# A hybrid RWKV-7 and short-convolution layer on one core: transposes on VectorE and ScalarE, elementwise work on GpSimd, and the first masked product behind the last scan

## The chip, the cores and the metric

One Trainium2 chip, one of its cores. The metric is the time of one execution in microseconds, the median over several runs. A profiled execution gives the trace. TensorE is called PE (its weight loads PEld), VectorE DVE, ScalarE ACT, GpSimd POOL, and SyncE, which issues most DMAs, SP.

## The reference

One inference step of one layer. 128 context tokens and 256 latent tokens, 384 in all, go through a modulated RMSNorm and one wide projection. Branch A is RWKV-7 time mixing with 32 heads of 64 channels, once in each direction; branch B is a gated convolution of width 3. Both are gated, projected, merged and projected again, and added to the input.

```python
def step(S, inp):                      # branch A, per head and direction
    r_t, w_t, k_t, v_t, a_t, b_t = inp
    sa = jnp.einsum('dbhij,dbhj->dbhi', S, a_t)
    S = S * w_t[..., None, :] + sa[..., :, None] * b_t[..., None, :] + v_t[..., :, None] * k_t[..., None, :]
    y = jnp.einsum('dbhij,dbhj->dbhi', S, r_t)
    return S, y
...
y_a = (y.astype(h.dtype) * jax.nn.silu(g_a)) @ w_out_a
u = _conv3_rows(c_gate * x_b, conv_w, rows)
y_b = (b_gate * u * jax.nn.silu(g_b)) @ w_out_b
merged = jax.nn.sigmoid(m_a) * y_a + jax.nn.sigmoid(m_b) * y_b
return merged @ w_o, S_fin
```

The context scan starts from zero and its final states are outputs; the latent scan starts from given states.

## The kernel before, in words

**The dense products.** All of them are done in float32 as three matmuls (`mm3`, lines 81 to 83): high part of the weights by high and low part of the activations, low part of the weights by the high part. A `wload` brings a block of weights (8 x 128 rows by 256 columns) and `split` makes its parts in two quarters, q = 0 and 1: ACT copies the high part (line 88) and DVE subtracts for the low part (line 89), 128x1024 each. `whi` and `wlo` have three buffers, `raw` two. One quarter feeds eight units; a unit is one `mm3`, three matmuls. The object `ds_` is the stream of all these products, and `ds_.go(n)` puts n units into PE's order. PE's order is written out by hand; that of the other engines is set by the tile scheduler, with priorities (`high_priority`) and bounds (`issue_after`). What a generator `yield`s in the head loop is the number of units that `drive` puts behind it.

**The head loop.** It runs over 16 pairs of heads, b = 0 to 15, called heads here; 128 channels are on the partitions, and 160 units of the stream stand beside each head in the steady state. For each head:

- `prep_a(b)`: decay and rate by low-rank products, the squared norm of the keys (`pn`, `kn`). `prep_k(b)`: inverse norm (`kn`, reciprocals), running sums of the logarithmic decay (`L`, a scan instruction on DVE), their exponentials `ep` and `em`, the keys `kd` and `bn`. It is issued inside the scan of the head before, by `keys`, behind the corner copies `turn`.
- `prep_b(b)`: the products `pr` (receptance and key by decay) and `bk` (lines 675 and 676), 14 units, then the masked product: `pA = bk x pr` for 6 chunks of 64 tokens, 2 heads and 2 directions, multiplied by a mask on DVE into `A` (line 709). The diagonal 32x32 triangles of A go by DMA to DRAM (`ui`) and back as `U` with one triangle on each of 48 partitions, are inverted there by 30 steps of elimination on DVE (two operations each, lines 724 and 726), and go back the same way (`uo`) into A. `x11` holds turned 32x32 blocks of it (line 737). On GpSimd, `bk` is multiplied by the decay of its chunk (line 716).
- `prep_c(b)`: PE turns the values (`pv`, line 763, 3 transposes for each direction) and the decayed keys (`pb`, line 772, 10 in all), and ACT copies the results into `sav` (line 765) and `bt` (line 773). The given states are loaded and turned.
- `scan(b)`: the two corner products `pH` and `pX` that complete the inverse with x11 (lines 842 and following), then two chains of steps, the context in 2 and the latents in 4 chunks. A step is `po` (state by pr), a sum into sav on DVE, `pq` (A by sav), a copy on ACT, `pu` (bt by sav) and the new state `st` on DVE (line 831 for a first context state, 833 for the others). At the end `py2` gathers the outputs into `ytok`.
- `norm(b)` (group norm over ytok, on DVE with a square on ACT and a power on GpSimd) and `finish(b)` (three transposes `py` on PE, scale on ACT, bonus and gate on DVE, lines 939 and 940, a store).

`prep_a` of the next head stands behind `prep_c`; finish of the head before stands between pr, bk and the masked product.

Of the kernel before, what the change touches and what calls it, by code (L numbers as in the profile page):

```python
# [56 lines left out]
def hybrid_step(ctx, tc, cst, x_prompt, x_sample, state_f, state_b, c, c_ctx, ada_w, ada_b, norm_g,  # L57
# [27 lines left out]
    def split(src, shape, th, tl, pool, nm, rows=P):  # L85
        hi = pool.tile(shape, F32R, tag=th, name=f"{th}_{nm}")
        lo = pool.tile(shape, F32R, tag=tl, name=f"{tl}_{nm}")
        S.copy(hi[0:rows], src)  # L88
        V.tensor_tensor(lo[0:rows], src, hi[0:rows].bitcast(F32), ALU.subtract)  # L89
# [4 lines left out]
    PRO, WINDOW, FIRST, LAST = 32, 80, 24, 16  # L94

    def wload(view, k0, cols, nm):

        w = P * len(cols)
        raw = wp.tile([P, 8, w], F32, tag="raw", name=f"raw_{nm}", bufs=2)
        if cols[-1] == cols[0] + P:  # L100
            nc.sync.dma_start(raw[:], view[:, k0:k0 + 8, cols[0]:cols[0] + 256])
        else:
            for i, c0 in enumerate(cols):
                nc.sync.dma_start(raw[:, :, i * P:(i + 1) * P], view[:, k0:k0 + 8, c0:c0 + P])
        res = [split(raw[:, 4 * q:4 * q + 4, :], [P, 4, w], "whi", "wlo", wp, f"{nm}_{q}") for q in range(2)]
        return res
# [501 lines left out]
    def prep_a(b, o):  # L608
# [58 lines left out]
    def prep_b(b, o):  # L667

        r, kk = r_[b], o["kk"]
        o["pr"], o["bk"] = [], []  # L670
        for d in range(2):
            ep, em, kd, bn = o["ep"][d], o["em"][d], o["kd"][d], o["bn"][d]
            pr = sp.tile([P, NCH, P], F32, tag=f"pr{d}", name=f"pr_{b}_{d}")
            bk = sp.tile([P, NCH, P], F32, tag=f"bk{d}", name=f"bk_{b}_{d}")
            V.tensor_tensor(bk[:, :, 0:C], c3(bn[:]), c3(em[:]), ALU.mult)
            V.tensor_tensor(bk[:, :, C:P], c3(kd[:]), c3(em[:]), ALU.mult)
# [20 lines left out]
        for d in range(2):  # L697
# [7 lines left out]
            for n0, w in ((0, 4), (4, 2)):  # L705
                mk = cs[:, m0:m0 + P].rearrange("p (w t) -> p w t", t=C).unsqueeze(1).broadcast_to([P, w, 2, C])
                for h in range(2):
                    f0 = NCH * d + n0
                    V.tensor_tensor(A[:, :, f0:f0 + w, hss[h]].rearrange("p w n t -> p n w t"),
                                    pas[h, n0][:, 0:w, :].rearrange("p n (w t) -> p n w t", t=C), mk, ALU.mult)  # L710
# [4 lines left out]
        for d in range(2):  # L715
            G.tensor_tensor(o["bk"][d][:], o["bk"][d][:], o["ep"][d][:, :, C:C + 1].broadcast_to([P, NCH, P]), ALU.mult)
# [19 lines left out]
        for d in range(2):  # L736
            box["turned"] = V.transpose(x11[0:32, 12 * d:12 * d + 12, :], blocks(A, d, 0)).ins

    def prep_c(b, o):

        r, v, A = r_[b], v_[b], o["A"]
# [9 lines left out]

        sav = sp.tile([P, 2 * NCH, P], F32, tag="sav", name=f"sav_{b}")
        bt = sp.tile([P, 2 * NCH, P], F32, tag="bt", name=f"bt_{b}")
        o["sav"], o["bkt"] = sav, bt
        for d in range(2):
            if d == 0:
                src = v
            else:
                src = tmp(f"vr_{b}")
                S.copy(src[:], v[:, ::-1])  # L760
            pv = bank(f"pv_{b}_{d}")
            for q in range(3):
                TE.transpose(pv[:, q, :], src[:, q * P:(q + 1) * P], ident)
            for e in range(2):
                S.copy(sav[C:P, NCH * d + e:NCH * d + NCH:2, :], pv[C * e:C * e + C, 0:3, :])
            yield 1
        for d in range(2):

            for n0, n1 in (((0, 4), (4, 5)), ((0, 3), (4, 6)))[d]:
                pb = bank(f"pb_{b}_{d}_{n0}")  # L770
                for n in range(n0, n1):
                    TE.transpose(pb[:, n - n0, :], o["bk"][d][:, n, :], ident)
                S.copy(bt[:, NCH * d + n0:NCH * d + n1, :], pb[:, 0:n1 - n0, :])
                yield 1
# [9 lines left out]
    def scan(b, o):  # L784
# [7 lines left out]
        def chain(ch):  # L792
            ls = None
            for i in range((2, 4)[ch]):
# [30 lines left out]
                if need_state:  # L825
# [3 lines left out]
                    for hs in hss:  # L829
                        if zero:  # L830
                            V.tensor_copy(st[ch][hs, :, hs], pu[hs, 0:2, hs])
                        else:
                            V.tensor_tensor(st[ch][hs, :, hs], pu[hs, 0:2, hs], ls[hs, :, hs], ALU.add)
# [125 lines left out]
    prep_k(0, cur)  # L959
    prev = None  # L960
    for b in range(NB):
# [210 lines left out]
```

## Time and profile before

| | us |
|---|---|
| median of 3 runs | 2238.54 |
| lowest and highest run | 2236.75, 2238.73 |
| the profiled execution, its own time | 2234.36 |
| its span in the trace | 2232.6 |
| PE busy in the span | 2173.1 |
| DVE busy | 1553.3 |
| ACT busy | 1013.5 |
| POOL busy | 115.7 |

The mean granted clock of PE was 0.998. Busy times of different engines overlap, so they don't add up to the span; matmul records overlap one another too, so a matmul's cost to PE is the distance from its start to the next one's. A row of the timeline gives the start and the duration in us, the engine, the line, the operation, what it writes and reads, and its shape; several instructions of one kind that follow one another are one row (x2, x3), and what is in brackets is the engine's idle time before it and what ended it. A row of the groups gives the count, the busy time in all and the mean of one in ns, and the engine's idle time before them.

### The profile page before, as it was taken

The numbers are of one execution on the slowest core, as the hardware profiler recorded it, in microseconds if no ns is written. First come the engines' busy times: TensorE is split into PE (matmuls) and PEld (weight loads), VectorE is DVE, ScalarE is ACT, GpSimd is POOL, SyncE is SP. The second block draws the span as 40 slices with busy tenths as digits, with TensorE's granted clock in tenths as the row PEclk, the third lists the DMA queues.
The fourth block names the chain that finished last, engine by engine and source line by source line (L and its number), as shares of the span: only waits on it lengthen the run. The fifth ranks groups of instructions, "written<-read, shape, count | busy, mean of one in ns | idle before, by whom it ended". The sixth has DMA issues, their size and how long they took to land.

```text
span 2232.6 us, 40518 instructions
## 1 busy us (share of the span) xinstructions
PE 2173.1 (97%) x16020; PEld 2062.7 (92%) x16020; DVE 1553.3 (70%) x3240; ACT 1013.5 (45%) x1784; POOL 115.7 (5%) x113
## 2 busy tenths in 40 slices
PE   5999999999999999999999999999999999999998
PEld 3589999999999999999999999999999999998988
DVE  3259567787878878777878787887777785444354
ACT  4245435454545454444445454546454633333333
POOL 2000000000000000000000000000000000000000
PEclk9999999999999999999999999999999999999999
DMA  9974454444343435343444434344445464886633
GB/s 338 346 211 128 131 141 116 116 117 118 108 132 107 130 100 131 106 130 100 121 108 127 112 107 133 107 122 126 124 118 139 144 196 143 294 281 233 220 132 113
DMA packets 426574, 335.25 MB, mean 150 GB/s; under 512 B 82496, under 2 KB 408720, under 8 KB 425488
## 3 DMA queue, kind: packets, MB, share of 16 engines
q1 hardware_dynamic: 424896, 330.91, 50.2%
q8 instruction: 126, 2.06, 0.4%
q10 hardware_dynamic: 432, 1.57, 0.2%
q14 instruction: 64, 0.52, 0.1%
q0 software_dynamic: 1056, 0.19, 0.1%
HBM read 305.80 MB, written 26.21 MB: 149 GB/s over the span
## 4 chain that ended last, share of the span: by engine, by line
PE 74%; DVE 12%; DMA 6%; ACT 4%; issue 2%; SPq 1%; POOL 0%; POOLq 0%; DVEq 0%; ACTq 0%
DMA raw_adah<-in_ada_w_dram 4%; PE d_rk L81 3%; PE d_rk L82 3%; PE d_rk L83 3%; PE d_gv L81 3%; PE d_gv L82 3%; PE d_gv L83 3%; PE d_oa L81 2%; PE pA L703 2%; PE d_oa L83 2%; PE d_oa L82 2%; PE d_mb L81 2%; PE d_mb L83 2%; PE d_mb L82 2%; PE d_bc L81 2%
## 5 line engine op out<-in xcount | busy, mean ns | idle before, releaser
L724 DVE TENSOR_TENSOR ut<-U 48x30 f32<-48x30 f32 (+14 forms) x480 | 154.8, 323 | 18.3 <-DMA U<-ui 5.5
L81 PE MATMUL d_rk<-h_hi,whi_rk 128*128 128x384 f32 x480 | 161.7, 337 | 0.6 <-ACT lst L554 0.6
L726 DVE TENSOR_TENSOR U<-U,ut 48x30 f32<-48x30 f32 (+14 forms) x480 | 154.5, 322 | 11.1
L81 PE MATMUL d_gv<-h_hi,whi_gv 128*128 128x384 f32 x480 | 160.6, 335 | 0.0
L82 PE MATMUL d_rk<-h_lo,whi_rk 128*128 128x384 f32 x480 | 160.5, 334 | 0.0
L83 PE MATMUL d_rk<-h_hi,wlo_rk 128*128 128x384 f32 x480 | 160.4, 334 | 0.0
L83 PE MATMUL d_gv<-h_hi,wlo_gv 128*128 128x384 f32 x480 | 160.4, 334 | 0.0
L82 PE MATMUL d_gv<-h_lo,whi_gv 128*128 128x384 f32 x480 | 160.4, 334 | 0.0
L88 ACT CAST whi_gv<-raw_gv 128x1024 fp32r<-128x1024 f32 (+1 forms) x64 | 64.0, 999 | 139.6 <-PE d_rk L82 100.0
L88 ACT CAST whi_rk<-raw_rk 128x1024 fp32r<-128x1024 f32 x60 | 63.0, 1054 | 110.8 <-PE d_rk L82 34.7
L89 DVE TENSOR_TENSOR wlo_rk<-raw_rk,whi_rk 128x1024 fp32r<-128x1024 f32 x60 | 72.9, 1218 | 45.3 <-ACT whi_rk L88 35.6
L81 PE MATMUL d_bc<-h_hi,whi_bc 128*128 128x384 f32 x256 | 92.2, 360 | 0.0
L81 PE MATMUL d_gb<-h_hi,whi_gb 128*128 128x384 f32 x256 | 92.2, 360 | 0.0
L81 PE MATMUL d_bg<-h_hi,whi_bg 128*128 128x384 f32 x256 | 92.2, 360 | 0.0
L81 PE MATMUL d_bx<-h_hi,whi_bx 128*128 128x384 f32 x256 | 92.1, 360 | 0.0
L81 PE MATMUL d_ma<-h_hi,whi_ma 128*128 128x384 f32 x256 | 91.6, 358 | 0.0
L81 PEld LDWEIGHTS d_rk<-h_hi,whi_rk 128*128 128x128 f32 x480 | 90.1, 188 | 0.9 <-ACT lst L554 0.9
L81 PE MATMUL d_mb<-h_hi,whi_mb 128*128 128x384 f32 x256 | 90.4, 353 | 0.0
L81 PEld LDWEIGHTS d_gv<-h_hi,whi_gv 128*128 128x128 f32 x480 | 90.1, 188 | 0.2
L81 PE MATMUL d_ob<-ybh,whi_ob 128*128 128x384 f32 x256 | 88.4, 345 | 2.0 <-DVE smb L521 1.0
L82 PEld LDWEIGHTS d_rk<-h_lo,whi_rk 128*128 128x128 f32 x480 | 90.2, 188 | 0.0
L82 PEld LDWEIGHTS d_gv<-h_lo,whi_gv 128*128 128x128 f32 x480 | 90.1, 188 | 0.0
(315 smaller groups left out, 6548.4 us busy)
## 6 DMA issues: line engine op xcount, KB each, us to landing
raw_adah<-in_ada_w_dram SPq DMA_DIRECT2D x64, 512.0 KB, 8.7
raw_rk<-in_w_in_dram SPq DMA_DIRECT2D x60, 512.0 KB, 5.3
raw_gv<-in_w_in_dram SPq DMA_DIRECT2D x60, 512.0 KB, 4.9
raw_ma<-in_w_in_dram SPq DMA_DIRECT2D x16, 1024.0 KB, 5.6
raw_mb<-in_w_in_dram SPq DMA_DIRECT2D x16, 1024.0 KB, 5.6
raw_bc<-in_w_in_dram SPq DMA_DIRECT2D x16, 1024.0 KB, 5.5
raw_bx<-in_w_in_dram SPq DMA_DIRECT2D x16, 1024.0 KB, 5.4
raw_bg<-in_w_in_dram SPq DMA_DIRECT2D x16, 1024.0 KB, 5.5
```

The source lines that it names most:

```text
L81: TE.matmul(out, wh, xh, start=start, stop=False)
L82: TE.matmul(out, wh, xl, start=False, stop=False)
L83: TE.matmul(out, wl, xh, start=False, stop=stop)
L88: S.copy(hi[0:rows], src)
L89: V.tensor_tensor(lo[0:rows], src, hi[0:rows].bitcast(F32), ALU.subtract)
L703: TE.matmul(pas[h, n // 4 * 4][:, n % 4, :], bk[hss[h], n, :], pr[hss[h], n, :], start=True, stop=True)
L724: V.tensor_tensor(tv, U[:, 0:s, s:s + 1].broadcast_to([48, s, w]), U[:, s:s + 1, s + 1:].broadcast_to([48, s, w]), ALU.mult)
L726: V.tensor_tensor(U[:, 0:s, s + 1:], U[:, 0:s, s + 1:], tv, ALU.add)
```

## The change

1. **Values.** `prep_v` turns v on DVE in 32x32 blocks (two instructions, 128x384), and 16 ACT copies of 32x192 put the blocks where they belong in sav. The transposes `pv` on PE, their copies and the copy of the reversed v are gone.
2. **Keys.** After GpSimd's decay, DVE turns bk in place in 32x32 blocks (two of 128x768), and 32 ACT copies of 32x192 place the blocks in bt. The transposes `pb` are gone.
3. **Low parts.** The second quarter (q = 1) of each wload has its low part made by GpSimd.
4. **Keys' decay.** `prep_p` makes the two halves of bk (by em) on GpSimd, for all heads but the first, issued behind the keys in the scan of the head before.
5. **pr** has two buffers; `prep_r` and `prep_v` of the next head are issued in the scan, behind the context chain's last state (`st0`).
6. **Joined.** The 14 units between pr and the masked product, and the one behind py2, are gone from the loop, so the next head's first masked product follows py2 directly. The norm of the head before is issued behind the masks, and 10 units and its finish follow the masked products.
7. **x11** shares one tile with U, and its turning is issued in the next head's prep_a.

```diff
+    def split(src, shape, th, tl, pool, nm, rows=P, eng=V):
...
-        V.tensor_tensor(lo[0:rows], src, hi[0:rows].bitcast(F32), ALU.subtract)
+        eng.tensor_tensor(lo[0:rows], src, hi[0:rows].bitcast(F32), ALU.subtract)
...
-    PRO, WINDOW, FIRST, LAST = 32, 80, 24, 16
+    PRO, WINDOW, FIRST, LAST, NRM = 32, 80, 24, 30, 10
...
-        res = [split(..., f"{nm}_{q}") for q in range(2)]
+        res = [split(..., f"{nm}_{q}", eng=(V, G)[q]) for q in range(2)]
...
+    def prep_v(b, o):
+        o["vt"] = []
+        for d in range(2):
+            x = sp.tile([P, T], F32, tag=f"vt{d}", name=f"vt_{b}_{d}")
+            V.transpose(x[:], v_[b][:, ::-1] if d else v_[b][:])
+            o["vt"].append(x)
+    def prep_p(b, o):
+        eng = G if b else V
...
+            eng.tensor_tensor(bk[:, :, 0:C], c3(o["bn"][d][:]), c3(o["em"][d][:]), ALU.mult)
+            eng.tensor_tensor(bk[:, :, C:P], c3(o["kd"][d][:]), c3(o["em"][d][:]), ALU.mult)
...
-        yield PB0
...
+        with tc.issue_after(last):
+            for d in range(2):
+                V.transpose(flat(o["bk"][d][:]), flat(o["bk"][d][:]))
...
+        ux = sp.tile([112, 1024], F32, tag="ux", name=f"ux_{b}")
+        U = ux[64:112].rearrange("p (a b) -> p a b", b=32)
...
+        for d in range(2):
+            for p in range(4):
+                for q in range(4):
+                    S.copy(bt[32 * p:32 * p + 32, NCH * d:NCH * d + NCH, 32 * q:32 * q + 32],
+                           o["bk"][d][32 * q:32 * q + 32, :, 32 * p:32 * p + 32])
+                yield 6
+        for d in range(2):
+            x = o["vt"][d][:].rearrange("p (n e t) -> p n e t", e=2, t=32)
+            for e in range(2):
+                for q in range(4):
+                    S.copy(sav[C + 32 * e:C + 32 * e + 32, NCH * d:NCH * d + NCH, 32 * q:32 * q + 32],
+                           x[32 * q:32 * q + 32, :, e, :])
+                yield 6
...
-        yield 1
+        yield 0
         V.tensor_tensor(ytok[:], ytok[:], py[:, 0:3, :], ALU.add)
...
         pb_gen = prep_b(b, cur)
-        ds_.go(next(pb_gen))
+        for d in range(2):
+            ds_.go(next(pb_gen))
         if prev is not None:
+            norm(b - 1, prev, cur["masked"])
+        drive(pb_gen)
+        n = 0
+        if prev is not None:
+            ds_.go(NRM)
+            n = NRM
             finish(b - 1, prev)
-        drive(pb_gen)
-        n = drive(prep_c(b, cur))
+        n += drive(prep_c(b, cur))
...
+        def values():
+            with tc.issue_after(cur["st0"]):
+                prep_r(b + 1, nxt)
+                prep_v(b + 1, nxt)
+        late = ((lambda: all(cur.get("turn", (None,))), keys), (lambda: "st0" in cur, values))
```

What stands in a row on the engines, by the order in which they get their instructions (a number behind a name is that of its buffer or its use):

On DVE, in a scan of the steady state, from the reciprocals of the next head's keys on. Before:

```order
L646 RECIPROCAL kn_7955<-kn_7955 128x128 x3
L654 SCALAR_TENSOR_TENSOR L_0_8105<-cs,sig_0_7896 128x384
L89 TENSOR_TENSOR wlo_bc_0_1_8046<-raw_bc_0_8039,whi_bc_0_1_8045 128x1024
L831 COPY st_1144<-pu_0_0_8143 64x2x64 x2
L647 SCALAR_TENSOR_TENSOR kn_7955<-kk_7860,kn_7955 128x384
L659 TENSOR_SCALAR kd_0_8109<-sig_2_7932,par,omka 128x384
L833 TENSOR_TENSOR st_1146<-pu_1_0_8159,ls_1_0_8031 64x2x64 x2
```

And now:

```order
L653 RECIPROCAL kn_8079<-kn_8079 128x128 x3
L661 SCALAR_TENSOR_TENSOR L_0_8231<-cs,sig_0_8020 128x384
L654 SCALAR_TENSOR_TENSOR kn_8079<-kk_7984,kn_8079 128x384
L666 TENSOR_SCALAR kd_0_8235<-sig_2_8056,par,omka 128x384
L661 SCALAR_TENSOR_TENSOR L_1_8239<-cs,sig_1_8032 128x384
L859 COPY st_1144<-pu_0_0_8275 64x2x64 x2
L667 TENSOR_TENSOR kd_0_8235<-k_7822,kd_0_8235 128x384
L668 TENSOR_TENSOR sig_2_8056<-kn_8079,sig_2_8056 128x384
L861 TENSOR_TENSOR st_1146<-pu_1_0_8291,ls_1_0_8157 64x2x64 x2
```

The low part of bc has left DVE, and the product of kn, kd and the second scan of the decay have moved ahead of the copies of the first context state.

On PE, at the end of that scan, where py2 (here py_5) gathers the outputs. Before:

```order
L82 MATMUL d_bc_1_8200<-h_lo_83,whi_bc_1_1_8207 128x384
L83 MATMUL d_bc_1_8200<-h_hi_79,wlo_bc_1_1_8208 128x384
L898 MATMUL py_5_8371<-sav_7533,A_7358 64x64 x24
L81 MATMUL d_bx_0_8396<-h_hi_76,whi_bx_0_0_8295 128x384
L82 MATMUL d_bx_0_8396<-h_lo_80,whi_bx_0_0_8295 128x384
```

And now:

```order
L82 MATMUL d_bc_1_8332<-h_lo_83,whi_bc_1_1_8339 128x384
L83 MATMUL d_bc_1_8332<-h_hi_79,wlo_bc_1_1_8340 128x384
L927 MATMUL py_5_8513<-sav_7499,A_7389 64x64 x24
L726 MATMUL pA_0_0_0_8555<-pr_0_8382,bk_0_8247 128x128
L726 MATMUL pA_0_1_0_8556<-pr_0_8382,bk_0_8247 128x128
```

The masked product of the next head has moved up to py2; it stood 15 units further on, behind the finish of the head before.

On GpSimd, from the decay of one head's bk to the clearing of A in its scan. Before:

```order
L716 TENSOR_TENSOR bk_1_7300<-bk_1_7300,ep_1154 128x768
L863 MEMSET A_7358 64x1536
L929 TENSOR_TENSOR rs_8434<-var_8431,nhalf 128x6
L716 TENSOR_TENSOR bk_0_8438<-bk_0_8438,ep_1148 128x768
L716 TENSOR_TENSOR bk_1_8444<-bk_1_8444,ep_1150 128x768
L863 MEMSET A_8502 64x1536
```

And now:

```order
L741 TENSOR_TENSOR bk_0_8247<-bk_0_8247,ep_1148 128x768
L741 TENSOR_TENSOR bk_1_8250<-bk_1_8250,ep_1150 128x768
L89 TENSOR_TENSOR wlo_bx_1_1_8584<-raw_bx_1_8577,whi_bx_1_1_8583 128x1024
L959 TENSOR_TENSOR rs_8654<-var_8651,nhalf 128x6
L89 TENSOR_TENSOR wlo_rk_0_1_8754<-raw_rk_0_8746,whi_rk_0_1_8753 128x1024
L89 TENSOR_TENSOR wlo_rk_1_1_8861<-raw_rk_1_8853,whi_rk_1_1_8860 128x1024
L89 TENSOR_TENSOR wlo_gv_0_1_8932<-raw_gv_0_8924,whi_gv_0_1_8931 128x1024
L89 TENSOR_TENSOR wlo_gv_1_1_9017<-raw_gv_1_9009,whi_gv_1_1_9016 128x1024
L89 TENSOR_TENSOR wlo_bg_0_1_9087<-raw_bg_0_9080,whi_bg_0_1_9086 128x1024
L89 TENSOR_TENSOR wlo_bg_1_1_9184<-raw_bg_1_9177,whi_bg_1_1_9183 128x1024
L892 MEMSET A_8554 64x1536
```

Seven low parts now stand on GpSimd between the decay and the clearing of A, around the power of the norm.

More of the change, by code (lines that the diff above doesn't have):

```diff
@@ L104, in wload @@
                 nc.sync.dma_start(raw[:, :, i * P:(i + 1) * P], view[:, k0:k0 + 8, c0:c0 + P])
-        res = [split(raw[:, 4 * q:4 * q + 4, :], [P, 4, w], "whi", "wlo", wp, f"{nm}_{q}") for q in range(2)]
+        res = [split(raw[:, 4 * q:4 * q + 4, :], [P, 4, w], "whi", "wlo", wp, f"{nm}_{q}", eng=(V, G)[q])
+               for q in range(2)]
         return res
@@ L636, in prep_a @@
         kn = sp.tile([P, T], F32, tag="kn", name=f"kn_{b}")
-        with tc.issue_after(box["turned"]) if "turned" in box else ExitStack():
+        if p is not None:
+            with tc.issue_after(lws):
+                p["turn_x"]()
+        with tc.issue_after(box["turned"]) if p is not None else ExitStack():
             box["kn"] = V.tensor_scalar(kn[:], pn, 1e-24, None, ALU.max).ins
@@ L734, in prep_b, with turn @@
                 nc.sync.dma_start(blocks(A, d, e), uo[d, e].rearrange("i s t -> s i t"))
-        for d in range(2):
-            box["turned"] = V.transpose(x11[0:32, 12 * d:12 * d + 12, :], blocks(A, d, 0)).ins
+        def turn():
+            for d in range(2):
+                box["turned"] = V.transpose(x11[0:32, 12 * d:12 * d + 12, :], blocks(A, d, 0)).ins
+        o["turn_x"] = turn
     def prep_c(b, o):
-        r, v, A = r_[b], v_[b], o["A"]
+        r = r_[b]
         s_in = sp.tile([P, 2, C], F32, tag="s_in", name=f"s_in_{b}")
@@ L750, in prep_c @@
                                       [:, :, 32 * jb:32 * jb + 32])
[L752 to L765, printed above, removed]
-            yield 1
[L767 to L774, printed above, removed]
         ks = o["kd"]
@@ L779, in prep_c @@
         yield 1
+        sav, bt = o["sav"], o["bkt"]
+        for d in range(2):
[4 more added lines that the diff above has]
+                yield 6
+        for d in range(2):
+            x = o["vt"][d][:].rearrange("p (n e t) -> p n e t", e=2, t=32)
[4 more added lines that the diff above has]
+                yield 6
         for h in range(2):
@@ L913, in scan, with norm @@
                                       nst[p0:p0 + 32, d, :].rearrange("i (b j) -> i b j", j=32))
-    def norm(b, o):
+    def norm(b, o, masked=None):
         ytok = o["ytok"]
@@ L919, in norm @@
         mu = sp.tile([P, 6], F32, tag="mu", name=f"mu_{b}")
-        V.tensor_reduce(mu[:], y6, AX.X, ALU.add)
+        with tc.issue_after(masked) if masked is not None else ExitStack():
+            V.tensor_reduce(mu[:], y6, AX.X, ALU.add)
         V.tensor_scalar(mu[:], mu[:], 1.0 / C, None, ALU.mult)
@@ L941, in finish, with drive @@
         nc.sync.dma_start(ya_d[b], ya[:])
-    def drive(gen, prio=0, at=None, fn=None):
-        n = i = 0
+    def drive(gen, prio=0, late=()):
+        n = 0
+        late = list(late)
         while True:
-            if i == at:
-                fn()
-            i += 1
+            for x in [x for x in late if x[0]()]:
+                x[1]()
+                late.remove(x)
             with tc.high_priority(offset=prio):
@@ L951, in drive @@
             if u is None:
+                assert not late
                 return n
@@ L967, in hybrid_step @@
         pb_gen = prep_b(b, cur)
-        ds_.go(next(pb_gen))
+        for d in range(2):
+            ds_.go(next(pb_gen))
         if prev is not None:
+            norm(b - 1, prev, cur["masked"])
+        drive(pb_gen)
+        n = 0
+        if prev is not None:
+            ds_.go(NRM)
+            n = NRM
             finish(b - 1, prev)
-        drive(pb_gen)
-        n = drive(prep_c(b, cur))
+        n += drive(prep_c(b, cur))
         nxt = {}
+        w = WINDOW + (FIRST if b == 0 else LAST if b == NB - 1 else 0)
         if b < NB - 1:
@@ L986, in keys @@
                 prep_k(b + 1, nxt)
-        drive(scan(b, cur), 300, 3 if b < NB - 1 else None, keys)
-        norm(b, cur)
+                prep_p(b + 1, nxt)
+        def values():
[3 more added lines that the diff above has]
+        late = ((lambda: all(cur.get("turn", (None,))), keys), (lambda: "st0" in cur, values))
+        drive(scan(b, cur), 300, late if b < NB - 1 else ())
         prev, cur = cur, nxt
+    norm(NB - 1, prev)
     ds_.go(12)
```

56 lines of the change are left out of this document (34 added, 22 removed).

## Prediction

> **What bounds the kernel now.** I read the page's busy shares and chain first, then stretches of the window view, then PE's waits inside the recurrence, and last the timelines of the stages that the change touches.
>
> ```profile
> span 2232.6 us, 40518 instructions
> PE 2173.1 (97%) x16020; PEld 2062.7 (92%) x16020; DVE 1553.3 (70%) x3240; ACT 1013.5 (45%) x1784; POOL 115.7 (5%) x113
> PE 74%; DVE 12%; DMA 6%; ACT 4%; issue 2%; SPq 1%; POOL 0%; POOLq 0%; DVEq 0%; ACTq 0%
> 600.00:800.00 200.00, 198.41 (x1574) 193.75 (x1573) 158.41 (x349) 92.69 (x166) 11.41 (x8) 1.00 0.43 116
> 746.08:775.33 29.25, 29.25 (x170) 29.25 (x170) 27.73 (x76) 11.27 (x14) 0.00 (x0) 1.00 0.39 112
> PE po L804 <- DVE st L833: 6.0, 8, 0.8
> PE pu L828 <- ACT sav L823: 1.2, 5, 0.3
> PE pq L821 <- DVE sav L805: 0.8, 2, 0.4
> ```
>
> PE is the bound: busy 97% of the span at a granted clock of 1.00, and 74% of the chain. In the middle of the head loop (the 200 us window; columns are length, then PE, PEld, DVE, ACT, POOL busy) it idles 1.6 us in 200. So an instruction taken from PE is time saved, and a wait put on PE is time lost. The last three rows are PE's waits in the scans between 300 and 1700 us, some thirteen heads: 8.0 us, 0.6 a head. DVE is no bound on average (79% of that window), but in the 29.25 us in which one head's triangular elimination runs it is busy 27.73 us, 95%: there is little room there for a DVE that is held up. POOL does nothing in that stretch.
>
> **Term 1: 16 transposes a head leave PE.**
>
> ```profile
> 737.18 0.33 PE L81 MATMUL d_bg<-h_hi,whi_bg 128*128 128x384 f32 x1
> 739.26 0.49 PE L763 MATMUL pv<-cs,v 128*128 128x128 f32 x3
> 743.81 0.34 PE L82 MATMUL d_rk<-h_lo,whi_rk 128*128 128x384 f32 x1
> ```
>
> Starts are pipelined, so a matmul costs its pitch and not its duration. From 737.18 to the first transpose at 739.26 stand 12 main matmuls: 2.08/12 = 0.1733 us each. From there to 743.81 stand all 16 transposes and 16 main matmuls: 4.55 - 16 x 0.1733 = 1.78 us. Sixteen heads make 28.4 us. PE's other work stays. Certain, if nothing else waits: **-28.4**.
>
> **What comes in its place on DVE, ACT and GpSimd.** The rows by line (count, busy us, mean ns):
>
> ```profile
> L716 POOL TENSOR_TENSOR bk<-bk,ep 128x768 f32<-128x768 f32 x32 | 49.3, 1541 | 155.6 <-PE pA L703 140.9 <-DMA ui<-A 10.1 <-issue 4.6
> L89 DVE TENSOR_TENSOR wlo_rk<-raw_rk,whi_rk 128x1024 fp32r<-128x1024 f32 x60 | 72.9, 1218 | 45.3 <-ACT whi_rk L88 35.6 <-DMA ma_d<-ma 4.5 <-DMA mb_d<-mb 4.5
> L676 DVE TENSOR_TENSOR bk<-kd,sig 128x384 f32<-128x384 f32 x32 | 17.5, 548 | 0.1
> L675 DVE TENSOR_TENSOR bk<-sig,sig 128x384 f32<-128x384 f32 x32 | 17.5, 548 | 0.0
> L737 DVE STREAM_TRANSPOSE x<-A 32x384 f32<-32x384 f32 x32 | 17.4, 558 | 25.3 <-DMA A<-uo 25.1
> L855 ACT COPY x<-pH 32x192 f32<-32x192 f32 x32 | 9.9, 311 | 46.6 <-PE pH L842 39.9 <-DVE x L855 6.7
> L765 ACT COPY sav<-pv 64x384 f32<-64x384 f32 x64 | 30.3, 474 | 15.0 <-PE pv L763 14.1
> L760 ACT COPY vr<-v 128x384 f32<-128x384 f32 x16 | 8.0, 502 | 0.0
> ```
>
> DVE turns: a turn of 384 columns took 0.558; taken by columns, two of 768 and two of 384 make 2 x 1.12 + 2 x 0.56 = 3.3 us a head. DVE gives up ten low parts (12.2 us) and four products (2.2 us), so it is 11 us lighter a head of 105. ACT: 48 copies of 32x192 at 0.311 = 14.9 us, less the sav copies (4 x 0.474) and vr (0.502), the old bt copies not counted: at most +12.5 us a head, from 46% of the window to 58%. The copies come in groups of four (1.2 us) with 6 units (3.1 us of PE) behind each, and at least 16 units of the next head's first preparation follow the last, so 8.3 us cover it. Cost taken: 0; with that cover gone, 1.2 us a head, 19 in all.
>
> GpSimd: no row shows its low part. Its 768-column product took 1.48 us at best (row below), 1.97 for 1024 columns; below it stands 1.22, DVE's own. I take 1.97. Ten low parts, four products and the two decays come to 10 x 1.97 + 4 x 0.74 + 2 x 1.54 = 26 us a head: far from a bound by itself.
>
> [...]
>
> **Who shuts out whom.** What the pages of groups don't show is that the two engines exclude one another:
>
> ```profile
> 185.25 1.48 POOL L716 TENSOR_TENSOR bk<-bk,ep 128x768 f32<-128x768 f32 x1 [36.71 <-PE pA L703]
> 185.66 3.28 DVE L89 TENSOR_TENSOR wlo_ma<-raw_ma,whi_ma 128x1024 fp32r<-128x1024 f32 x2
> 304.59 1.49 POOL L716 TENSOR_TENSOR bk<-bk,ep 128x768 f32<-128x768 f32 x1 [5.21 <-PE pA L703]
> 304.62 0.68 DVE L709 TENSOR_TENSOR A<-pA,cs 128x512 f32<-128x512 f32 x1
> 305.22 1.27 DVE L940 TENSOR_TENSOR ya<-ya,ga 128x384 f32<-128x384 f32 x1
> 191.37 2.38 POOL L716 TENSOR_TENSOR bk<-bk,ep 128x768 f32<-128x768 f32 x1 [4.65 <-issue]
> ```
>
> Two low parts took 3.28 instead of 2 x 1.22 where POOL was running; the ya product 1.27, where such a product takes 0.55, so it began at about 305.94, 0.14 before POOL's recorded end. The masked product, which reads PSUM, took 0.68 beside POOL and wasn't held. And a POOL product that came second took 2.38 instead of 1.48. So a DVE operation with two operands in SBUF and a POOL operation wait for one another, whole instructions long.
>
> [...]
>
> Per low part moved DVE gains 1.22 and may lose 1.97 - 0.14 = 1.83. Where DVE has slack that is nothing. Two places have none.
>
> **Term 2: the scan.** The first scan steps of head 5, with the next head's keys already on DVE:
>
> ```profile
> 794.76 2.55 DVE L646 RECIPROCAL kn<-kn 128x128 f32<-128x128 f32 x3
> 796.32 1.05 ACT L88 CAST whi_bc<-raw_bc 128x1024 fp32r<-128x1024 f32 x1 [0.27 <-PE d_gb L82]
> 797.25 0.88 DVE L654 TENSOR_TENSOR_SCAN L<-cs,sig 128x384 f32<-128x384 f32 x1
> 798.06 1.19 DVE L89 TENSOR_TENSOR wlo_bc<-raw_bc,whi_bc 128x1024 fp32r<-128x1024 f32 x1
> 799.27 0.59 DVE L831 COPY st<-pu 64x128 f32<-64x128 f32 x2
> 799.90 0.56 DVE L647 SCALAR_TENSOR_TENSOR kn<-kk,kn 128x384 f32<-128x384 f32 x1
> 800.37 0.48 DVE L659 TENSOR_SCALAR kd<-sig,par,omka 128x384 f32<-128x384 f32 x1
> 800.78 0.60 PE L804 MATMUL po<-st,pr 128*128 128x128 f32 x4
> ```
>
> This low part is one of those moved. Its cast ends at 797.37; GpSimd starts when the L scan lets go, at about 798.0, and holds till 798.0 + 1.97 - 0.14 = 799.8. In the new order of DVE the kn product, kd and the second L scan stand ahead of the state copies. kn has two SBUF operands, so it starts at 799.8; then by pitches 0.47 + 0.51 + 0.81 + 0.62 to the end of the copies: 802.2. po, for which PE wants the states, stands at 800.78: 1.4 us of PE waiting. What is behind po on PE is the feed, so it all waits. Fourteen heads have this order (the first has another feed, the last no next head): **+19.6**. Bounds: 0, if GpSimd got in earlier or kn isn't held, to 2 us x 15 = 30, had it to run after the kn product too. The rows above speak for holding.
>
> The second place is the r products and v turns behind the context's last state: 4 x 0.55 + 2 x 0.56 = 3.3 us of DVE, which the next sav add may find in its way by up to 0.5 us. Before's own waits there (0.6 us a head) came from the kd and bn products that now run elsewhere. **0**, bounds -8 and +8.
>
> **Term 3: the elimination.** From the mask to the corner product pH, head 5 and then head 4:
>
> ```profile
> 735.68 1.95 DVE L709 TENSOR_TENSOR A<-pA,cs 128x512 f32<-128x512 f32 x4 [0.65 <-PE pA L703]
> 746.08 0.18 DVE L724 TENSOR_TENSOR ut<-U 48x30 f32<-48x30 f32 x1 [0.30 <-DMA U<-ui]
> 775.12 0.20 DVE L726 TENSOR_TENSOR U<-U,ut 48x30 f32<-48x30 f32 x1
> 782.78 1.14 DVE L737 STREAM_TRANSPOSE x<-A 32x384 f32<-32x384 f32 x2 [1.40 <-DMA A<-uo]
> 787.37 0.62 PE L842 MATMUL pH<-x,A 32*32 32x32 f32 x48
> 681.65 1.02 DVE L737 STREAM_TRANSPOSE x<-A 32x384 f32<-32x384 f32 x2 [2.15 <-DMA A<-uo]
> 682.37 0.76 PE L842 MATMUL pH<-x,A 32*32 32x32 f32 x48
> ```
>
> Masked at 737.63, U ready to use at 746.08 (8.45 later), eliminated at 775.32, back and turned at 783.92; pH at 787.37, a slack of 3.4 us. Head 4 has none: pH begins as the second turn ends. In the new order the mask comes 15 units earlier before the scan (14 of the feed, one of the last scan): +7.8, less the 1.78 of transposes, plus 0.3 for finish's transposes, now inside: +6.3 us of time. Against it: the norm and the ya products now stand ahead of U, by which I let it start 1.9 us later (bounds 0 and 4); the bk turns, 2.2; four low parts leave DVE, -4.9; four or five GpSimd low parts block it, 4.4 x 1.83 less the DVE idle of 1.5 already there: +6.6. Together 5.8 against 6.3: the slacks stay about what they are. The three heads with none (4, 8 and 15 by the same two rows) take 1 us each: **+3**, bounds 0 and +15.
>
> The norm now runs behind the mask, and finish's transposes 10 units behind; the norm's eight steps, at 0.55 as the products above, take some 5 us, and 16 units from the first masked product (8.3 us) are there. 0, and 0.5 us a head if they are late.
>
> **Sum.** -28.4 + 19.6 + 0 + 3 = -5.8 on a profiled execution of 2234.36 us (span 2232.6): 2228.6. The median of the runs, 2238.54, is 0.19% above that execution, so on that scale **2233**.
>
> **Rivals.**
> - The elimination decides: slower. If U's stretch ends 4 us later than worked (two or three GpSimd operations more inside it, or U starting behind the GpSimd products), the slacks of 0 to 3.8 us are spent in every head; over the heads that is some 30 us of PE waiting at pH. Speaking for it is the 95% of the stretch, against it the 11 us of lighter DVE. 2228.6 + 27: **2260**, between 2245 and 2275. It turns from harmless where x11 ends behind pH's place, 56 us after the mask. Chance 0.35.
> - Nothing visible waits: GpSimd finds DVE's gaps, and the states come in time. -28.4 with nothing against it: 2206, on the median's scale **2210**, and to 2220 with half of term 2. For it speaks the 20% of DVE's time that is idle; against it that the state copies stand behind the hoisted kn. Chance 0.18.
> - ACT is late: whi casts wait behind groups of four copies, the first pu behind bt, 1.2 us a head as above: 2233 + 19 = **2252**. For it speaks that the copies are spread over the whole preparation, against it that ACT would still idle 42%. Chance 0.12.
> - My sum, 10 us to either side by term 2 at half or one and a half of 1.4 us: 2222 to 2243. Chance 0.35.
>
> About 0.2%, 4.5 us, is what a measurement of this kernel can tell from no change. Faster, below 2234: all of the second rival, two thirds of my sum: 0.43. Same: a third of my sum, little of the others: 0.19. Slower 0.38. The range runs from 2210 to 2260: what is left out is the upper half of the elimination's case.
>
> **What would show it.** L763 and L772 gone from PE and the pitch unbroken there; L89 on POOL at about 2 us; in the scan PE waiting at po for DVE's state copy, 1.4 us a head, with a POOL low part just ahead; pH's waits on x short in most heads. I am wrong if po doesn't wait (faster), if pH waits several us a head (slower), or if GpSimd's low part isn't within 1.2 to 2.4 us.

## The result, and the profile after

The changed kernel takes 2461.06 us (median of 4 runs, 2457.85 to 2462.33) against 2237.68 before: 1.0996 times, 95% interval 1.0977 to 1.1015. It is 10% slower where 0.2% faster was forecast. The page, and the same stretch of both kernels in the window view (before, then after):

```profile
span 2456.0 us, 40810 instructions
PE 2223.3 (91%) x15764; PEld 2088.1 (85%) x15764; DVE 1642.7 (67%) x3054; ACT 1204.3 (49%) x2396; POOL 681.4 (28%) x363
PE 45%; DVE 37%; ACT 7%; DMA 5%; issue 4%; SPq 1%; POOL 1%; DVEq 0%; POOLq 0%; ACTq 0%
```

```profile
300.00:1700.00 1400.00, 1391.94 (x10892) 1359.83 (x10891) 1098.03 (x2407) 682.99 (x1238) 77.14 (x54) 1.00 0.43 119
```

```profile
300.00:1700.00 1400.00, 1265.11 (x9453) 1219.83 (x9451) 1064.70 (x2024) 744.45 (x1544) 428.84 (x211) 0.96 0.38 105
```

PE's share of the chain fell from 74% to 45%, and DVE's rose from 12% to 37%. In 1400 us PE idles 135 us instead of 8, and its mean granted clock is 0.96 instead of 1.00. 190 low parts, 232 us at 1.22, went from DVE to GpSimd, and DVE's busy time did not go down: 1642.7 against 1553.3. PE's largest waits after, from 200 us on (a row gives who waited for whom, us in all, how often, and the longest; "pq" waits for the sum into sav):

```profile
PE d_gv L83 <- DVE wlo_gv L89: 63.6, 24, 4.5
PE po L832 <- DVE st L859: 25.9, 14, 1.9
PE po L832 <- DVE st L861: 18.4, 10, 2.1
PE py L966 <- DVE ytok L960: 13.1, 14, 1.0
PE d_rk L81 <- DVE bg L487: 12.1, 3, 4.1
PE pq L849 <- DVE sav L833: 9.9, 13, 1.4
```

All six are for DVE. No wait of PE in the trace is for GpSimd, and none is at pH, where I looked for the elimination's lateness. What PE waits for most is the *first* quarter's low part, the half that stayed on DVE. Head 5 shows why (ACT, POOL, DVE and PE rows of the timeline, put in one fence in the order of reading):

```profile
936.28 1.05 ACT L88 CAST whi_gv<-raw_gv 128x1024 fp32r<-128x1024 f32 x1 [1.49 <-issue]
941.58 2.52 POOL L89 TENSOR_TENSOR wlo_gv<-raw_gv,whi_gv 128x1024 fp32r<-128x1024 f32 x1 [4.12 <-ACT whi_gv L88]
941.88 2.48 DVE L759 TENSOR_TENSOR ut<-ux 48x228 f32<-48x228 f32 x1
946.13 1.23 DVE L89 TENSOR_TENSOR wlo_gv<-raw_gv,whi_gv 128x1024 fp32r<-128x1024 f32 x1
947.41 0.44 PE L83 MATMUL d_gv<-h_hi,wlo_gv 128*128 128x384 f32 x1 [2.36 <-DVE wlo_gv L89]
```

The cast of this quarter ended at 937.33. Behind it DVE still had 15 operations to do, 12 of them the elimination's, before its low part, in the fixed order of the queue. One took 2.48 instead of 0.39, because GpSimd was running the other quarter (941.58 to 944.10). So the low part began 8.8 us after its cast, and PE waited 2.36 us. From the last mask to the end of the elimination DVE needs 53.5 us, where it needed 38.8 (means of twelve heads, from the timelines).

GpSimd holds up more forms than I had allowed for. Groups before (first fence) and after:

```profile
L659 DVE TENSOR_SCALAR kd<-sig,par,omka 128x384 f32<-128x384 f32 x32 | 14.8, 462 | 0.0
L921 DVE TENSOR_SCALAR mu<-mu 128x6 f32<-128x6 f32 x16 | 2.7, 169 | 0.3
```

```profile
L666 DVE TENSOR_SCALAR kd<-sig,par,omka 128x384 f32<-128x384 f32 x32 | 47.0, 1470 | 0.5
L951 DVE TENSOR_SCALAR mu<-mu 128x6 f32<-128x6 f32 x16 | 24.7, 1541 | 0.0
L970 DVE TENSOR_TENSOR ya<-ya,ga 128x384 f32<-128x384 f32 x16 | 36.1, 2259 | 0.5
```

The tensor_scalar forms, with one tensor input, were held as well (kd from 0.46 to 1.47, and mu from 0.17 to 1.54 for 6 columns). The ya product went from 0.60 to 2.26.

And the clock. A wait, and what the matmuls behind it take:

```profile
959.85 0.69 PE L83 MATMUL d_gv<-h_hi,wlo_gv 128*128 128x384 f32 x1 [3.82 <-DVE wlo_gv L89]
960.33 0.52 PE L81 MATMUL d_gv<-h_hi,whi_gv 128*128 128x384 f32 x1
960.65 0.52 PE L82 MATMUL d_gv<-h_lo,whi_gv 128*128 128x384 f32 x1
...
963.00 0.34 PE L81 MATMUL d_gv<-h_hi,whi_gv 128*128 128x384 f32 x1
963.17 0.33 PE L82 MATMUL d_gv<-h_lo,whi_gv 128*128 128x384 f32 x1
```

From 959.31 to 962.72 the granted clock was 0.50, and the pitch there is 0.32 instead of 0.173. 28 such stretches begin between 200 and 2000 us, 122.9 us in all, and none in the kernel before. Some 324 matmuls of 128x384 start in them; at 0.32 for 0.173 they lose about 47 us. With 172 us more waiting (all idle time ahead of PE's instructions, 223.1 against 50.8) less the 28.4 us of transposes that makes 191 of the 223 us; the rest is not attributed.

### The profile page after: what moved, and what is told of

It is laid out like the page before. It is cut to its first block, busy times and chain, and to the rows that moved or that the text cites. A ratio compares the mean times of both kernels' runs of the same rounds, so it can differ in the third digit from the quotient of the medians.

```text
span 2456.0 us, 40810 instructions
## 1 busy us (share of the span) xinstructions
PE 2223.3 (91%) x15764; PEld 2088.1 (85%) x15764; DVE 1642.7 (67%) x3054; ACT 1204.3 (49%) x2396; POOL 681.4 (28%) x363
## 4 chain that ended last, share of the span: by engine, by line
PE 45%; DVE 37%; ACT 7%; DMA 5%; issue 4%; SPq 1%; POOL 1%; DVEq 0%; POOLq 0%; ACTq 0%
DVE ut L759 7%; DVE ux L761 6%; ACT bt L798 3%; DMA raw_adah<-in_ada_w_dram 3%; PE d_oa L81 2%; PE d_gv L83 2%; PE d_oa L83 2%; PE d_oa L82 2%; DVE kd L666 2%; PE d_gv L81 2%; PE d_gv L82 2%; DVE kn L653 2%; PE pA L726 2%; DVE ya L970 1%; DVE wlo_gv L89 1%
## 5 line engine op out<-in xcount | busy, mean ns | idle before, releaser
L83 PE MATMUL d_gv<-h_hi,wlo_gv 128*128 128x384 f32 x480 | 173.7, 362 | 63.6 <-DVE wlo_gv L89 63.6
L759 DVE TENSOR_TENSOR ut<-ux 48x30 f32<-48x30 f32 (+14 forms) x480 | 214.3, 446 | 19.1 <-DMA ux<-ui 3.0
L761 DVE TENSOR_TENSOR ux<-ux,ut 48x30 f32<-48x30 f32 (+14 forms) x480 | 193.7, 404 | 15.7
L798 ACT COPY bt<-bk 32x192 f32<-32x192 f32 x512 | 179.0, 350 | 20.7 <-DVE bk L746 13.8
L83 PEld LDWEIGHTS d_gv<-h_hi,wlo_gv 128*128 128x128 f32 x480 | 98.3, 205 | 71.3 <-DVE wlo_gv L89 71.3
L89 POOL TENSOR_TENSOR wlo_gv<-raw_gv,whi_gv 128x1024 fp32r<-128x1024 f32 (+1 forms) x32 | 76.2, 2381 | 231.4 <-ACT whi_gv L88 231.4
L89 POOL TENSOR_TENSOR wlo_rk<-raw_rk,whi_rk 128x1024 fp32r<-128x1024 f32 x30 | 79.2, 2640 | 216.5 <-ACT whi_rk L88 178.2
L81 PEld LDWEIGHTS d_rk<-h_hi,whi_rk 128*128 128x128 f32 x480 | 95.1, 198 | 24.7 <-DVE bg L487 13.1
L83 PEld LDWEIGHTS d_rk<-h_hi,wlo_rk 128*128 128x128 f32 x480 | 94.8, 198 | 3.5 <-DVE wlo_rk L89 3.4
L837 ACT ACTIVATE ls<-st,ep 128x128 f32<-128x128 f32 x128 | 46.0, 396 | 100.1 <-DVE st L861 47.3
L805 ACT COPY sav<-vt 32x192 f32<-32x192 f32 x256 | 89.2, 348 | 9.1 <-PE py L927 6.0
L83 PE MATMUL d_ob<-ybh,wlo_ob 128*128 128x384 f32 x256 | 89.0, 348 | 4.9 <-DVE wlo_ob L89 4.9
```

The source lines that it names most:

```text
L81: TE.matmul(out, wh, xh, start=start, stop=False)
L83: TE.matmul(out, wl, xh, start=False, stop=stop)
L89: eng.tensor_tensor(lo[0:rows], src, hi[0:rows].bitcast(F32), ALU.subtract)
L759: V.tensor_tensor(tv, U[:, 0:s, s:s + 1].broadcast_to([48, s, w]), U[:, s:s + 1, s + 1:].broadcast_to([48, s, w]), ALU.mult)
L761: V.tensor_tensor(U[:, 0:s, s + 1:], U[:, 0:s, s + 1:], tv, ALU.add)
L798: S.copy(bt[32 * p:32 * p + 32, NCH * d:NCH * d + NCH, 32 * q:32 * q + 32], o["bk"][d][32 * q:32 * q + 32, :, 32 * p:32 * p + 32])
```

## The experiments

"Before" is the kernel before, run beside each. Theory A: GpSimd's operations over SBUF shut DVE out (the expectations call that the lock). Rival B: the new order and ScalarE's copies.

**GpSimd's work taken back.** Edits of the changed kernel: `eng=V` for all low parts (first run), and also `eng = V` in prep_p (second run).

> The changed kernel with all low parts of the weights back on VectorE; keys' decay on GpSimd, turned values and keys, and the joined order stay. Theory A (GpSimd's products over SBUF shut VectorE out; what is late on VectorE in the elimination and the scan then delivers the weights' low parts late): most of the loss goes, 2250 to 2320 us; the waits of d_gv and d_rk on low parts go from about 65 us to under 15. Rival B (the loss lies in the new order: the norm, the turns and ScalarE's 48 copies ahead of and inside the elimination): VectorE now has 10 x 1.2 us more a head, so it stays above 2400 or gets slower than 2461.

> The changed kernel with the low parts and the keys' decay both back on VectorE; turned values and keys, and the joined order stay. Theory A: GpSimd is nearly idle again; 2210 to 2250 us, the waits at po under 10 us in all. Rival B: above 2400 us, with the same waits of d_gv on low parts.

2309.25 us, 1.0317 [1.0300, 1.0334], and 2298.51, 1.0269 [1.0254, 1.0284]. The low parts alone are 152 of the 223 us, the keys' products 11, and PE's waits for wlo_gv fell from 63.6 us to 3.7. DVE's busy time with 190 low parts more is 1641.8, the same as without them: 232 us of work had left it, and as much waiting had come. But some 60 us stay, more than A forecast for the second run.

**GpSimd's work added to the kernel before.** First half of the low parts on GpSimd, then instead of that a dummy, then fills:

```diff
+        res = [split(..., eng=(V, G)[q]) for q in range(2)]              # first run
+        for j in range(2):                                                # second run, nobody reads dum
+            G.tensor_tensor(dum[:], raw[:, 4 + 2 * j:6 + 2 * j, :], raw[:, 2 * j:2 * j + 2, :], ALU.subtract)
+        G.tensor_copy(dum[:, 0:1], raw[:, 7, 0:1])                        # third run
+        for j in range(5):
+            G.memset(dum[:], 0.0)
```

> The kernel before with one change: half of the low parts (q = 1) on GpSimd. Theory A: four or five GpSimd operations of 2.4 us fall into each elimination, of which VectorE had 1.5 us idle; net 3 to 6 us late a head, 2290 to 2360 us, with some slow-clock spells. Rival B: VectorE is 12 us a head lighter and the old order is kept, so 2225 to 2245 us.

> The kernel before, and for each block of weights GpSimd makes two subtractions of 128x512 from the raw weights into a scratch tile that nobody reads. The results don't change; VectorE keeps all its work and no engine waits for GpSimd's result, but for the raw buffer. Theory A: some ten times 2 x 1.2 us of lock a head, 8 to 10 us of it in the elimination: 2330 to 2430 us. Rival B, and any reading by which GpSimd's late result is what costs: 2238 us, within 10.

> The kernel before, and for each block of weights one GpSimd copy of a single column of the raw weights and behind it five GpSimd fills of 128x512, about 2.6 us together, as long as the two subtractions of the dummy run before. Results don't change. Theory A in its narrow form (VectorE is shut out by GpSimd operations that read SBUF): 2238 to 2260 us, what the one-column copies cost. Theory A in a wide form (any GpSimd operation on SBUF shuts it out): 2380 to 2430.

2449.80 us, 1.0945 [1.0928, 1.0961]; 2416.60, 1.0800 [1.0782, 1.0818]; 2240.74, 1.0017 [1.0007, 1.0027]. Busy times of the dummy run and of the fills:

```profile
PE 2229.5 (93%) x16020; PEld 2094.7 (87%) x16020; DVE 1772.1 (74%) x3240; ACT 1012.3 (42%) x1784; POOL 739.4 (31%) x493
```

```profile
PE 2177.2 (97%) x16020; PEld 2065.8 (92%) x16020; DVE 1559.8 (70%) x3240; ACT 1012.9 (45%) x1784; POOL 740.8 (33%) x1253
```

The first run lies far above A's own figure, and its PE waits for what stands on DVE in and behind the elimination, the low parts wlo_gv (47.2 us) and lwl (those of the low-rank weights, 34.2), not at pH. POOL is equally busy in the other two, 740 us. Where it reads SBUF, DVE's same 3240 instructions take 219 us longer than before and the kernel 8%. Where it only fills, DVE takes 6 us longer and the kernel 0.2%. One product of the elimination (U<-U,ut 48x238) takes 395 ns before, 609 beside the dummy and 395 beside the fills; the whole elimination takes 30.4, 38.5 and 30.5 us (means of twelve heads). That is theory A in its narrow form for operations with two inputs, and nothing of the change is in these two kernels. The dummy also holds the raw blocks longer, and ScalarE's casts wait for some of them, but the elimination reads none. The tensor_scalar operations, with one input, did wait for fills, but there are few of them (mu took 346 ns on average, 169 before):

```profile
L925 DVE TENSOR_SCALAR mu<-mu 128x6 f32<-128x6 f32 x16 | 5.5, 346 | 0.3
```

**What is left: turned or joined?** From the second run above, the order taken apart (14 units and the norm before the masks again, first run), and PE's transposes put back (second run).

> Values and keys turned by VectorE and placed by ScalarE as in the changed kernel, GpSimd as before, and the order not joined: 14 units between py2 and the masked product, the norm before the masked product, finish ahead of it, groups of copies 5 units apart instead of 6 so that a head keeps its 160 units. If the 60 us that are left without GpSimd's new work come from the joined order (norm, turns and bk copies all between mask and elimination): 2205 to 2225 us, the 28 us of the transposes gained. If they come from the turns and copies themselves: 2270 to 2300.

> The joined order alone: PE's transposes of values and keys stay, GpSimd as before, x11 turned in the next head's first preparation, norm behind the masks, finish 10 units later. If the joined order costs: 2270 to 2300 us, with py waiting for the norm's last product. If the turns and copies cost: 2230 to 2245.

2337.18 us, 1.0448 [1.0433, 1.0464], and 2276.49, 1.0181 [1.0161, 1.0202]. The first lies above both of its expectations; the second is where it should be if the join costs, but without a wait of py. Each half costs by itself, both with U where the change had put it. In all of these traces operations of the elimination had lost their overlap with others. The same three operations before (first fence), and with U moved to partitions 64 to 111 (from the run that follows):

```profile
868.06 0.39 DVE L726 TENSOR_TENSOR U<-U,ut 48x238 f32<-48x238 f32 x1
868.38 1.21 DVE L89 TENSOR_TENSOR wlo_gv<-raw_gv,whi_gv 128x1024 fp32r<-128x1024 f32 x1
869.51 0.39 DVE L724 TENSOR_TENSOR ut<-U 48x234 f32<-48x234 f32 x1
```

```profile
884.61 0.40 DVE L726 TENSOR_TENSOR U<-U,ut 48x238 f32<-48x238 f32 x1
885.05 1.23 DVE L89 TENSOR_TENSOR wlo_gv<-raw_gv,whi_gv 128x1024 fp32r<-128x1024 f32 x1
886.31 0.40 DVE L724 TENSOR_TENSOR ut<-U 48x234 f32<-48x234 f32 x1
```

Before, the next start comes 0.07 us ahead of the end (868.06 + 0.39 against 868.38), now 0.04 behind it: 0.11 us at each change, some 33 a head, 3.5 us in the stretch that is 95% busy. Part 7 of the change had moved U there to share a tile with x11.

```diff
-        ux = sp.tile([112, 1024], F32, tag="ux", name=f"ux_{b}")
-        U = ux[64:112].rearrange("p (a b) -> p a b", b=32)
+        ux = sp.tile([64, 1024], F32, tag="ux", name=f"ux_{b}")
+        U = ux[0:48].rearrange("p (a b) -> p a b", b=32)         # ut likewise; x11 stays on 0 to 63
```

The first run moves U and ut to 64 in the kernel before, the other three move them to 0 in the joined and turned kernel, in the turned one and in the changed one:

> The kernel before with one change: U and its scratch ut lie on partitions 64 to 111 instead of 0 to 47, as in the changed kernel. Nothing is added or moved. Theory C (where U lies costs: in the traces with U on 64 to 111, VectorE's change between an operation of the elimination and another takes 0.03 us from end to start, where before the next one starts 0.075 us ahead of the end; 0.11 us x some 33 changes a head = 3.5 us): the slack of 0 to 3.8 us before pH is spent, 2250 to 2300 us, and the changes show +0.03. Rival D (the loss of overlap comes from the new order or from sharing the tile with x11): 2238, and the changes show -0.075.

> Turned values and keys and the joined order, all of GpSimd's new work back on VectorE, and U on partitions 0 to 47 of the tile that it shares with x11 (on 0 to 63). Theory C: 2220 to 2255 us against 2299 with U on 64 to 111. Rival D: 2299.

> Turned values and keys in the old, not joined order, without GpSimd's new work, U on partitions 0 to 47. Theory C: the transposes' 28 us show at last, 2205 to 2250 us against 2337 with U on 64 to 111. Rival D, or the turns and copies themselves: above 2300.

> The changed kernel whole, GpSimd's new work too, with U on partitions 0 to 47. Theory C with theory A: 3.5 us a head less on VectorE in the elimination, where it is behind; 2370 to 2420 us. If the lock alone decides: 2440 to 2460.

2275.93, 1.0172 [1.0157, 1.0187]; 2255.49, 1.0078 [1.0063, 1.0093]; 2275.44, 1.0174 [1.0157, 1.0191]; 2399.69, 1.0725 [1.0696, 1.0754]. Theory C holds: 38 us added to the kernel before, and 43, 62 and 61 taken from the others; rival D falls. In the first run the elimination takes 34.4 us instead of 30.4, and PE waits for lwl (10.1 us) and for ga, a gate's product on DVE (16.7), more than at pH (1.6), where C had looked. But the turned kernel in the old order still loses 38, where C had it at 2250 at most; PE waits 22.5 us for lwl there.

**The wait of py.** The joined and turned kernel with U on 0, and finish 14 units behind the masks instead of 10. The wait there before this edit, and the largest that are new after it:

```profile
PE py L966 <- DVE ytok L960: 23.6, 14, 4.4
```

```profile
PE d_rk L81 <- DVE bg L487: 4.7, 3, 1.6
PE d_rk L83 <- DVE wlo_rk L89: 3.1, 3, 1.1
```

> Turned values and keys, joined order, GpSimd as before, U on partitions 0 to 47 (2255 us), and finish of the head before 14 units behind the masked products instead of 10, with the four groups of value copies 5 units apart instead of 6, so that a head keeps its units. If the waits of py on the norm's last product (23.6 us in that run's trace) were what kept it above the kernel before: 2228 to 2236 us, py's waits under 3 us, faster than before by up to 0.4%. If the time is set by something behind it (the copies on ScalarE, the elimination): 2250 to 2256 us and another wait in py's place.

2247.93 us, 1.0039 [1.0025, 1.0053]. py's waits are nearly gone (2.4 us in all), but the kernel gains only 7.6 of the 23.6 us. About half of it came back as new waits of d_rk for DVE (10.8 us in all); those for bu and bc (6.1 each) and one of 8.0 at the end stood there before this edit and stay. Taken back in this order, against the kernel before beside each run, the 223 us have become 71, 60, 18 and 9.

**Values, keys and join, each alone**, with U on 0 and GpSimd as before.

> The kernel before with the values alone turned by VectorE (behind the masks) and placed by 16 ScalarE copies; keys still turned on PE, old order, GpSimd as before, U and x11 sharing a tile with U on partitions 0 to 47. PE loses 6 transposes a head, about 11 us in all. If turns of this size fit VectorE's waits between mask and elimination: 2226 to 2234 us. If any added VectorE or ScalarE work in this stretch is paid for on PE: 2240 to 2255.

> The kernel before with the keys alone turned by VectorE in place and placed by 32 ScalarE copies; values on PE, old order, keys' products in their old place behind the scan. PE loses 10 transposes a head, about 17 us. If the turns and copies are what cost in the version with all turned (2275 us): 2245 to 2270 us. If the keys' products, which that version makes inside the scan, are what cost there: 2220 to 2232.

> The joined order alone (PE's transposes, GpSimd as before) with U on partitions 0 to 47. Theory C: back from 2276 to about 2238 us, and what stays above is the price of the keys' products inside the scan, where the consumers of the stream on VectorE come late (2240 to 2250). If the join itself costs: 2255 to 2276.

2245.66, 1.0041 [1.0029, 1.0054]; 2276.32, 1.0174 [1.0160, 1.0188]; 2261.94, 1.0109 [1.0094, 1.0125]. The first lies in its higher range, the second above both of its ranges, the third in its higher range, so turns and join both cost. The keys turned alone lose 39 us although PE saves 17 there, and with the keys' products in their old place.

```profile
PE pl L83 <- DVE lwl L89: 18.4, 16, 3.8
PE pH L843 <- DVE x L740: 7.0, 8, 3.0
```

PE waits for lwl, which stands close behind the elimination in DVE's queue, and for x11. The elimination itself takes hardly longer there (30.9 us against 30.4 before), but it starts later: 11.5 us behind the last mask instead of 8.4 (means of twelve heads). ScalarE is in it. The low parts of rk stand ahead of U in DVE's queue, and the casts that they need stand behind the keys' copies (a row of ScalarE; DVE's waits for these casts before, then here):

```profile
537.94 4.69 ACT L778 COPY bt<-bk 32x192 f32<-32x192 f32 x13
```

```profile
DVE wlo_rk L89 <- ACT whi_rk L88: 35.6, 21, 4.5
```

```profile
DVE wlo_rk L89 <- ACT whi_rk L88: 76.2, 28, 5.8
```

The join costs 25 us without any turning: pv waits for ACT, and the stream for consumers on DVE, as above.

```profile
PE pv L794 <- ACT vr L791: 9.5, 15, 4.8
PE d_gb L81 <- DVE bu L481: 6.0, 3, 2.0
```

With the values alone, the norm is late for py in six heads:

```profile
PE py L938 <- DVE ytok L932: 9.5, 6, 3.4
```

**A version that gains.** The values alone, their turns bound to come behind the masks, and finish behind both masked products. The second part of the edit:

```diff
         ds_.go(next(pb_gen))
+        ds_.go(next(pb_gen))
+        ds_.go(next(pb_gen))
         if prev is not None:
             finish(b - 1, prev)
```

> The version with the values alone turned (2246 us), with the turns held back until the masks are done, and finish of the head before put behind the two masked products instead of ahead of them. In that run's trace six waits of py on the norm (9.5 us, up to 3.4 in heads 4 and 8) and a first scan 5 us later stood against the 11 us that PE saves. If these were all: 2226 to 2233 us, faster than before by 0.2 to 0.5%. If the added ScalarE and VectorE work costs by itself: 2238 to 2248, with other waits in their place.

2234.11 us against 2238.70, 0.9982 [0.9973, 0.9991]: faster by 0.2%, less than the low end of the expectation.

```profile
PE pl L83 <- DVE lwl L89: 3.6, 3, 1.8
PE pb L768 <- DVE A L709: 2.8, 1, 2.8
```

No wait of py is left, and these are the largest that the kernel before did not have. From one head's first pav product to the next's, heads 12 and 13 take 103.7 us where they took 104.4, which is the 0.7 us of six transposes. Of the parts that were run alone, it is the only one that pays, and only with finish moved.

## Why the prediction was wrong, point by point

- **Term 1 (transposes): right.** In the later-finish run heads 12 and 13, in which PE has 0.2 us of waits, last 102.67 us where they lasted 104.40 and 104.37: 1.7 a head, 1.78 forecast.
- **GpSimd's price: too low, from the wrong row.** I scaled the decay's 1.48 us for 768 columns to 1.97. The decay's second operand is one column broadcast, and it took 1.93 ns a column; the low part reads two streams, and where nothing held it, it took 2.39 us, 2.33 ns a column:

```profile
911.42 2.39 POOL L89 TENSOR_TENSOR wlo_bx<-raw_bx,whi_bx 128x1024 fp32r<-128x1024 f32 x1 [0.57 <-ACT whi_bx L88]
```
- **Term 2 (scan): mechanism right, a quarter too small.** In the scan of head 5, DVE, POOL and PE:

```profile
868.73 3.46 POOL L89 TENSOR_TENSOR wlo_bc<-raw_bc,whi_bc 128x1024 fp32r<-128x1024 f32 x1 [8.56 <-ACT whi_bc L88]
869.29 0.52 DVE L654 SCALAR_TENSOR_TENSOR kn<-kk,kn 128x384 f32<-128x384 f32 x1
869.74 2.67 DVE L666 TENSOR_SCALAR kd<-sig,par,omka 128x384 f32<-128x384 f32 x1
873.28 0.59 DVE L859 COPY st<-pu 64x128 f32<-64x128 f32 x2
874.02 0.68 PE L832 MATMUL po<-st,pr 128*128 128x128 f32 x4 [1.85 <-DVE st L859]
```

  The kn product slipped in ahead; the kd tensor_scalar was held instead, which I had counted as free. po waited 1.85 us, 25.9 in 14 heads, against 1.4 and 19.6. With the low parts back on DVE this wait is gone. At my second place, costed at 0 with 8 as its bound, PE waited 28 us, for the later states (18.4) and the sav adds (9.9), where it had waited 8 before. With the keys' products back on DVE as well, both waits fall to 4.4 and 0.4: what held DVE there was GpSimd's keys' products, whose hold on DVE I had not placed, and not the r products and turns that I had weighed.
- **Term 3 (elimination): the step that failed.** I summed 5.8 us of lateness from the mask to the end of the elimination; it was 14.7 (53.5 against 38.8), some 4 of it from U's partitions, which I had left out. And I put it to pH alone, as an excess over a slack, at +3 us. DVE took its operations in the order of its queue (15 of them between head 5's cast of gv and its low part, 8.8 us), and the low parts and the stream's consumers stand between the elimination's steps. They were late first, so PE stopped at d_gv (63.6 us) and d_rk (24.3) and never came early to pH. The rival that the elimination decides had the right engine, but at +30 it too counted only pH.
- **U's partitions: a step that I left out.** The shared tile is in my description of the change and not in its costs. 38 us on the kernel before, 61 on the changed one.
- **Norm, finish, keys' products in the scan: costed at 0.** py waits 13.1 us in the changed kernel and 23.6 without GpSimd's work; the join alone, with all three in it, costs 25.
- **The clock: not in the sum.** 47 us that no wait shows, since the waits were costed at their length.
- **ACT: costed at 0.** The rival that ACT is late had late casts behind the groups of copies, at 1.2 us a head. In the keys' run they are there, and the elimination starts 3.1 us later. The keys' copies were never run without the keys' turns; how the 56 us that the keys lose divide between the two stays open.

## What to carry to other kernels

Work moved to GpSimd was not taken off DVE here, where both read SBUF: 190 low parts went and DVE's busy time stayed the same (1642.7 us without them, 1641.8 with them). In a stretch where DVE was 95% busy, what was added came late to all that stood behind it in the queue (PE waited 63.6 us for the low parts of gv), so look for what the bound engine takes from that queue first, and not only at the end of the chain. Count a moved tile's start partition (38 us on the kernel before), and after each wait that you forecast on PE the slow matmuls behind it (some 47 us here).

## What the runs showed of the hardware that I had not expected

- Beside GpSimd's operations DVE's fp32 tensor_scalar was held too (mu, 6 columns, from 0.17 to 1.54 us). DVE's 64x64 block transposes (0.24 beside GpSimd's low parts and products and without, 32 each) and its operations with a PSUM operand (0.55 and 0.55, 12 of ga beside them) weren't held. GpSimd's fills held tensor_scalar as well (mu from 0.17 to 0.35), but not the product of the elimination, with two inputs (0.395 and 0.395; 740 us of GpSimd's time, most of it fills, cost the kernel 0.2%).
- A DVE operation on partitions from 64 on didn't overlap with one from 0 on: in the two stretches above it began 0.04 us behind the other's end, where with both from 0 on it began 0.07 ahead of it, 0.11 us for each change.
- PE's clock went to half after short waits, by a fixed beat. In the changed kernel the 28 stretches with a granted clock of 0.50 last 3.41 us or two or three times that, and all begin on one grid of 3.41 us. In the 3.41 us ahead of each, PE had idled at least 1.81. From the full clock, no step of the grid with less than 1.80 idle led to one (in two other runs one each came after 1.61 and 1.33). Two steps of the grid, first with a wait of 1.85 us that lies whole in one, then with 1.72 of a wait of 2.09 (the columns are those of the window view, the granted clock third from the right):

```profile
993.44:996.85 3.41, 1.56 (x11) 1.27 (x10) 3.32 (x7) 1.31 (x4) 0.99 (x2) 1.00 0.55 138
996.85:1000.27 3.42, 3.42 (x14) 3.34 (x13) 3.34 (x10) 2.50 (x7) 2.75 (x3) 0.50 0.49 169
```

```profile
884.22:887.63 3.41, 1.69 (x10) 1.37 (x8) 3.29 (x7) 0.12 (x1) 2.38 (x1) 1.00 0.11 16
887.63:891.05 3.42, 3.01 (x18) 2.72 (x19) 3.33 (x8) 1.05 (x3) 0.00 (x0) 1.00 0.57 139
```
